# Longer expert lists in a two-layer decoder kernel, with rows of `v` copied beside their weights ahead of time

## The chip, the cores and the metric

The kernel runs on one core of a Trainium2 chip. The metric is the device time of one execution in microseconds, as the median of several runs. Seven names recur: TensorE (PE in the profile; PEld is its weight load), VectorE (DVE), ScalarE (ACT), GpSimd (POOL), SyncE (SP), and the DMA queues of SyncE, ScalarE and GpSimd (q1, q10 and q0 in the profile's list of queues).

## What is computed

The reference is a decoder trunk of two layers on 256 tokens of width 1024, all in float32. Layer 0 mixes tokens with a Mamba-2 style scan (SSD), layer 1 with block-sparse causal attention (MoBA). Behind each mixer stands a layer norm, then a mixture of very many small experts (PEER), another layer norm and a gated embedding add. The change is in the expert part:

```
def block(xb):                                   # 128 tokens
    q = (xb @ w_q).reshape(128, 8, 2, 128)       # 8 heads
    s = einsum('thcd,hcnd->thcn', q, sub_keys)   # scores against 2 x 128 keys
    ...                                          # 16 best pairs of keys per head
    expert = ...                                 # index in 0..16383
    gate = softmax(best, axis=-1)
    act = gelu(einsum('td,thkd->thk', xb, u[expert]))
    return einsum('thk,thkd->td', gate * act, v[expert])
```

Each token uses 8 x 16 = 128 of the 16384 experts. An expert has a row of `u` and a row of `v`, 1024 numbers each, in each layer.

## The kernel before, in words

**Columns.** The 16384 experts are 128 columns of 128. For every column the kernel loads the 512 KB block of `u`, splits it into a high and a low float32r part (`split`, L124: one ScalarE copy at L126, one VectorE subtraction at L127), and computes the activations of all 128 experts for all 256 tokens on TensorE (`expert_in`, L915). The gates are spread into the same shape on TensorE (`spread`, L978), where a further matmul for each token also counts which experts of the first `MANY` = 92 columns are used at all (L993), and multiplied in. Columns 0 to 91 lie in one SBUF tile, `act`, the other 36 in another, `high`.

**Output.** The output is the sum over experts of weight times row of `v`. The last 36 columns are *dense*: the whole 512 KB block of `v` is loaded by SyncE, split, and multiplied (`expert_out`, L170). A product of two split numbers takes three passes, so a dense column is 3 passes x 2 token blocks x 2 halves of the width = 12 matmuls of 512 columns (`mm3s`, L149, matmul at L152). The first 92 columns are *listed*: of their experts only those that some token uses are taken, in groups of 128. There are three kinds: used by both token blocks (12 matmuls a group), by the first only, by the second only (6 each). `CAPS` gives the number of groups that the program has for each kind: 37, 22 and 22. What does not fit raises a flag, and a fallback loop (`general`, L1212, called by `branch`) then does the surplus.

**How a group is fetched.** ScalarE's queue writes the weights of the listed columns to DRAM (`keep`, L1009): both token blocks to the table `w_d`, rows of 256 numbers, and the first block alone to `a_d`, rows of 128. For each group GpSimd then issues two indirect DMAs (`fetched`, L1175, issue at L1189): one gathers the 128 rows of weights (from `a_d` for the kind "first block only", else from `w_d`), one the 128 rows of `v`. Both are split (`group_load`, L1195) and multiplied (`group_out`, L1203).

**The listing.** `listing` (L1032) turns the counts into the row numbers for the gathers: it makes the three classes, running sums over columns (`sums`), ranks (`ranks`, L1089, two matmuls), places in the list (`places`, L1094), one equality mask and 8 tiny matmuls for each 8 columns (`place`, L1106), then sorts each row's list with rounds of "8 largest, remove them" (`order`, L1134) and computes the row numbers (`rows`, L1142). Most of it is on VectorE, and it runs beside the last 12 `expert_in` and the first `LEAD` = 6 dense columns (L1262 to L1271).

**Order of the work.** Everything is written out by position. `spread_over` gives each step of a list a place between 0 and 1, and `emit` merges the lists. The first group stage holds the 22 groups of the first block and the next `MIX` = 13 dense columns (L1290). The second holds the "both" groups, the "second block" groups, 14 dense columns, and the loads for the layer's end (L1313). Behind it come 3 held-back dense columns and the last `TAIL` = 2 groups, so that the norm of token block 0 can begin early. `pace.marks` and `after` only fix the order on an engine's queue; they add no wait.

**Buffers.** Loaded blocks go round 4 buffers `raw`, split blocks round 4 buffers `hl` (both 128 x 1024). The second group stage gathers into 6 buffers `raws` and 8 `rows_w`, which take the place of `act`.

**The mixers.** `chunk` (L132) is the way in for every weight block: a 512 KB load by SyncE and its split. The SSD mixer takes 52 chunks before layer 0's expert part, the attention mixer 30 in its own stage; then the expert part's query stage takes 16 (`query`).

## Time and profile before

Three runs took 1823.28, 1824.83 and 1824.98 us, median 1824.83. The profiled execution took 1825.7 us, of which the program's span is 1823.9 us.

| | before |
|---|---|
| profiled execution / span | 1825.7 / 1823.9 us |
| granted TensorE clock, mean | 0.999 |
| HBM read / written | 364.98 / 42.50 MB |
| layer 0's last output matmuls end near | 927 us |
| layer 1's last output matmuls end near | 1796 us |

| stage (us) | what runs |
|---|---|
| 0 to 241 | SSD mixer, then the queries of layer 0 |
| 241 to 640 | activations and gates of layer 0 |
| 640 to 680 | last activations, listing, first dense columns |
| 680 to 926 | the two group stages of layer 0 |
| 926 to 1130 | end of layer 0, attention mixer, queries of layer 1 |
| 1130 to 1497 | activations and gates of layer 1 |
| 1497 to 1545 | last activations, listing, first dense columns |
| 1545 to 1796 | the two group stages of layer 1 |
| 1796 to 1824 | end of layer 1 |

How to read the profile's rows. A group of instructions has its line, engine and operation, the tile written and the tiles read, the count, then busy time and the mean duration of one in ns, then the idle time of its engine just before them and what ended it; "issue" is idle time in which nothing that the profile shows was waited for. A row by stage has start and end, the length, then the busy time of each engine with its number of instructions, the granted clock, the share of time that the 16 DMA engines were busy (packets of several queues can overlap, so it can pass 1) and GB/s. A row of a chain of waits has a start, a length and what the time was spent on, followed back from the last instruction. A row of one line's instructions has shortest, median and longest duration in ns and the first and last start in us. A row of waits has who waited for whom, us in total, how often, and the longest.

### The profile page before, as it was taken

The page shows a single profiled execution, that of the slowest core. Times are in us where ns is not written, and L with a number is a line of the kernel's source. Part 1 is how long each engine was busy: PE and PEld are TensorE (multiplying, and loading weights), DVE is VectorE, ACT ScalarE, POOL GpSimd, SP SyncE. Part 2 cuts the span into 40 slices and gives each one's busy share as a digit, 9 for nine tenths or more (in the row PEclk, how much of TensorE's full clock was granted, in tenths as well). Part 3 has the DMA queues.
Part 4 walks back from the last instruction along what each step waited for, and adds up shares of the span by engine and source line. Part 5 has one row for each costly group of instructions (what it writes and reads, how often), then busy time and mean ns, then how long its engine had stood idle before and what let it go on. Part 6 is the DMA issues. An engine that isn't in the chain of part 4 may idle for free.

```text
span 1823.9 us, 31779 instructions
## 1 busy us (share of the span) xinstructions
PE 1806.1 (99%) x11152; PEld 1543.8 (85%) x11152; DVE 1493.5 (82%) x2948; ACT 1155.7 (63%) x2326; POOL 629.4 (35%) x608
## 2 busy tenths in 40 slices
PE   8999999999999999999999999999999999999999
PEld 7998888888888888788888788888888888887887
DVE  7798789988988997666667878998898899776675
ACT  6865556697665766565646655669666666665563
POOL 0011003332222247777700000333222224777770
PEclk9999999999999999999999999999999999999999
DMA  7655669898799998988836656989879999898880
GB/s 249 221 188 183 215 177 227 222 230 216 185 253 323 280 328 301 316 308 305 286 132 192 198 195 177 228 218 233 214 180 259 327 268 331 303 319 286 313 298 34
DMA packets 214890, 443.17 MB, mean 243 GB/s; under 512 B 18916, under 2 KB 123528, under 8 KB 213064
## 3 DMA queue, kind: packets, MB, share of 16 engines
q1 hardware_dynamic: 76360, 270.94, 45.7%
q0 software_dynamic: 66560, 133.99, 28.1%
q10 hardware_dynamic: 71808, 36.18, 6.9%
q8 instruction: 88, 1.44, 0.3%
q14 instruction: 74, 0.61, 0.1%
HBM read 364.98 MB, written 42.50 MB: 223 GB/s over the span
## 4 chain that ended last, share of the span: by engine, by line
PE 46%; DVE 4%; issue 3%; POOL 2%; ACT 2%; DMA 1%; POOLq 0%; DVEq 0%; ACTq 0%
PE acc L152 18%; PE acc L168 17%; PE acc L156 5%; PE mm L168 2%; POOL raw L1189 1%; DVE hl L127 1%; PE aux L992 1%; DMA raw<-in_v,r 1%; POOL rows_w L1189 1%; ACT hl L126 1%; PE mm L993 1%; PE mm L992 1%; PE aux L800 0%; DMA raw<-in_u 0%; DVE high L836 0%
## 5 line engine op out<-in xcount | busy, mean ns | idle before, releaser
L127 DVE TENSOR_TENSOR hl<-raw,hl 128x1024 fp32r<-128x1024 f32 x574 | 699.3, 1221 | 197.0 <-ACT hl L126 190.5
L168 PE MATMUL acc<-xT,hl 128*128 128x256 f32 (+1 forms) x4608 | 841.0, 340 | 1.5 <-DVE xT L195 0.8
L168 PEld LDWEIGHTS acc<-xT,hl 128*128 128x128 f32 x4608 | 701.1, 188 | 101.2 <-DVE hl L127 4.1
L126 ACT CAST hl<-raw 128x1024 fp32r<-128x1024 f32 x574 | 602.1, 1052 | 210.8 <-DMA raw<-in_v,r 105.3
L152 PE MATMUL acc<-hl,w 128*128 128x512 f32 x2196 | 502.2, 390 | 3.5 <-ACT hl L126 2.4
L152 PEld LDWEIGHTS acc<-hl,w 128*128 128x128 f32 x2196 | 412.5, 188 | 92.4 <-ACT hl L126 3.8
L932 POOL DMA_DIRECT2D w<-w x160 | 139.1, 869 | 400.1 <-ACT w L951 247.5
L932 POOL DMA_DIRECT2D act<-w x96 | 83.6, 871 | 302.8 <-ACT w L931 181.8
L1189 POOL DMA_INDIRECT raw<-in_v,r x132 | 153.4, 1162 | 40.2 <-issue 32.6
L930 ACT COPY w<-acc 128x256 f32<-128x256 f32 x160 | 59.8, 374 | 164.8 <-PE acc L168 159.7
L1189 POOL DMA_INDIRECT rows_w<-w_d,r x118 | 141.7, 1201 | 36.0 <-issue 32.0
L156 PE MATMUL mm<-xT,hl 128*128 128x256 f32 x816 | 100.9, 284 | 1.8 <-ACT hl L126 1.1
L156 PEld LDWEIGHTS mm<-xT,hl 128*128 128x128 f32 x816 | 98.6, 192 | 3.3 <-ACT hl L126 1.6
L931 ACT COPY w<-acc 128x256 f32<-128x256 f32 x256 | 97.3, 380 | 0.0
L930 ACT COPY act<-acc 128x256 f32<-128x256 f32 x96 | 35.7, 372 | 68.5 <-PE acc L168 68.1
L976 DVE TENSOR_TENSOR pick<-pick,r 128x2048 f16<-128x2048 f16 x64 | 78.2, 1222 | 0.9
L992 PEld LDWEIGHTS <-pick 128*128 128x128 f16 x1024 | 66.7, 98 | 14.3 <-issue 11.3
L221 POOL TENSOR_TENSOR ln_s<-ln_s,mhalf 128x1 f32<-128x1 f32 x8 | 4.4, 550 | 185.7 <-PE acc L156 130.6
L993 PE MATMUL mm<-pick 128*128 128x92 f16 x512 | 68.1, 204 | 0.0
L543 POOL TENSOR_TENSOR sq<-sq,sqt 128x256 f32<-128x256 f32 x12 | 12.5, 1040 | 150.2 <-ACT sqt L542 150.0
L992 PE MATMUL aux<-pick 128*128 128x128 f16 x688 | 59.6, 220 | 1.4 <-ACT high L1005 1.2
L1189 POOL DMA_INDIRECT pick<-a_d,r x44 | 52.2, 1187 | 14.9 <-issue 11.6
(298 smaller groups left out, 2133.2 us busy)
## 6 DMA issues: line engine op xcount, KB each, us to landing
raw<-in_u SPq DMA_DIRECT2D x256, 512.0 KB, 4.7
raw<-in_v SPq DMA_DIRECT2D x72, 512.0 KB, 5.3
w_d<-act ACTq DMA_DIRECT2D x44, 512.0 KB, 7.3
w<-w POOLq DMA_DIRECT2D x160, 128.0 KB, 5.6
raw<-in_w_q SPq DMA_DIRECT2D x32, 512.0 KB, 3.8
raw<-in_w_xbc SPq DMA_DIRECT2D x24, 512.0 KB, 4.1
act<-w POOLq DMA_DIRECT2D x96, 128.0 KB, 5.3
a_d<-act ACTq DMA_DIRECT2D x22, 512.0 KB, 10.2
```

The lines of the kernel that those rows point to most:

```text
L126: a = self.nc.scalar.copy(hi, src)
L127: b = self.nc.vector.tensor_tensor(lo, src, hi.bitcast(F32), op=OP.subtract)
L152: self.last_mm = self.nc.tensor.matmul(out, lhs(a), rhs(b), start=start and i == 0, stop=stop(n) and i == 2).ins
L156: self.last_mm = self.nc.tensor.matmul(out, lhs(a), rhs(b), start=start and i == 0, stop=stop and i == 2).ins
L168: self.nc.tensor.matmul(dst, hl[:, a, k * P:(k + 1) * P], src, start=k + a == 0, stop=(k, a) == order[-1] and k == KD - 1)
L930: nc.scalar.copy(whole, pe[:, :T])
L931: copied = nc.scalar.copy(pair[:, 1, :], pe[:, T:]).ins
L932: nc.gpsimd.dma_start(whole, pair[:, 1, :], accum_op=OP.add)
L976: nc.vector.tensor_tensor(a2, both, gates, op=OP.mult)
L992: nc.tensor.matmul(pg[:, t, :], one[:, 0, 4 * h + t], a2[:, 4 * h + t, k], start=k == 0, stop=k == 1)
L993: nc.tensor.matmul(banks["used"][:, MANY * tb:MANY * tb + MANY], one[:, 0, 4 * h + t], a2[:, 4 * h + t, 0, :MANY], start=at == 0, stop=at ...
L1189: got = nc.gpsimd.indirect_dma_start(out=dst, out_offset=None, in_=src, in_offset=rows(which))
```

## The change

The constants `MANY`, `CAPS` and `BASES` go, and each layer gets a plan: the number of listed columns, the number of *staged* columns among them, the groups of each kind, and how many of these groups are *fixed*, that is, filled from the staged columns alone:

| | listed | staged | groups (both, first, second) | fixed among them | dense columns |
|---|---|---|---|---|---|
| before, both layers | 92 | 0 | 37, 22, 22 | 0 | 36 |
| after, layer 0 | 96 | 16 | 38, 23, 23 | 6, 3, 3 | 32 |
| after, layer 1 | 104 | 40 | 42, 25, 25 | 15, 8, 8 | 24 |

For a staged column the table in DRAM has rows of 1280 numbers: the 1024 of `v`, then the 256 weights. The `v` part is copied from `v` to the table, DRAM to DRAM, 512 KB a column, on ScalarE's DMA queue (`stage`). `staging` spreads the copies over the chunks of the mixers: 16 for layer 0 over 46 chunks from the 24th chunk of the program on, 40 for layer 1 over 44 chunks from the start of the attention mixer. A fixed group then needs one gather of 5 KB rows where it needed two. In the listing, where a staged class has fewer experts than its fixed groups have room for, later ranks are moved up by the shortfall (`short`), and `order` sorts the staged and the other columns apart. A group beyond the fixed ones can still hold staged experts, so its row numbers are converted to the table's narrow rows (`rows`).

Around it: `raws` grow to rows of 1280, the tile `half` is dropped and the last group's split pair is put into two of the four `raw` buffers instead, layer 1 holds four gate matrices rather than three in the new pool, and the routing's scratch in layer 1 lies in `act`, since `high` has become too small for it.

```diff
-MANY = 92
-CAPS = (37, 22, 22)
-BASES = (0, 37, 59)
-GROUPS = sum(CAPS)
+PLANS = ((96, 16, (38, 23, 23), (6, 3, 3)), (104, 40, (42, 25, 25), (15, 8, 8)))
+WIDE = D // T + 1
...
+    def staged(self, i):
+        return self.w_d[i][:(PLANS[i][1] * P + 1) * WIDE].rearrange("(n f) t -> n (f t)", f=WIDE)
+
+    def stage(self, i, c):
+        self.nc.scalar.dma_start(self.staged(i)[1 + c * P:1 + c * P + P, :D], self.dram["v"][i, c])
+
+    def spare(self):
+        self.chunks += 1
+        while self.copies and self.chunks * self.per_copy >= self.copied + 1:
+            self.copied += 1
+            with self.after(self.pace.marks):
+                self.copies.pop(0)()
+
+    def staging(self, i, first, chunks):
+        n = PLANS[i][1]
+        self.copies = [lambda c=c: self.stage(i, c) for c in range(n)]
+        self.chunks, self.copied, self.per_copy = -first, 0, n / chunks
...
+        self.spare()
         return hl
...
                     nc.tensor.matmul(pr, every, pad[1][:, :, 64:], start=False, stop=True)
+                    if STAGED:
+                        picked["total"] = bank[:, 3 * MANY:3 * MANY + 3]
+                        nc.tensor.matmul(picked["total"], every, pad[1][:, :, 64 + STAGED], start=True, stop=True)
...
+                    if STAGED:
+                        for k in range(3):
+                            V.tensor_scalar(short[:, k:k + 1], picked["total"][:, k:k + 1], -1.0, float(FIXED[k] * P),
+                                            op0=OP.mult, op1=OP.add)
+                        V.tensor_scalar(short, short, 0.0, None, op0=OP.max)
+                        V.tensor_tensor(r[:, :, STAGED:], r[:, :, STAGED:],
+                                        short[:, :, None].to_broadcast([P, 3, MANY - STAGED]), op=OP.add)
...
                 def order(k):
-                    src = key[:, k]
-                    for n in range(0, wide[k], 8):
-                        top = best[k][:, n:n + 8]
-                        V.max(top, src)
-                        if n + 8 < wide[k]:
-                            V.match_replace(out=src, in_to_replace=top, in_values=src, imm_value=-3e38)
+                    f = FIXED[k]
+                    for hi, at, n in ((STAGED, 0, f), (MANY, f, CAPS[k] - f)):
+                        src = key[:, k, :hi]
+                        for j in range(0, n, 8):
+                            top = best[k][:, at + j:at + j + 8]
+                            V.max(top, src)
+                            if hi == STAGED or j + 8 < n:
+                                if hi == STAGED and n - j < 8:
+                                    V.memset(top[:, n - j:], 3e38)
+                                V.match_replace(out=src, in_to_replace=top, in_values=src, imm_value=-3e38)
...
-                    V.tensor_scalar(picked["w"][:, s], ids[:, s], -2.0 if k == 2 else -1.0, 1.0 if k == 2 else 0.0,
-                                    op0=OP.mult, op1=OP.add)
...
+                    near = s if k == 1 else fixed
+                    if near.start < near.stop:
+                        V.tensor_scalar(picked["w"][:, near], ids[:, near], -1.0, None, op0=OP.mult)
+                    if k != 1:
+                        at = mark[:, free]
+                        V.tensor_scalar(at, ids[:, free], 1.0 - WIDE, WIDE - 1.0, op0=OP.mult, op1=OP.add)
+                        V.scalar_tensor_tensor(at, at, float(AT - STAGED * P - 1), ids[:, free], op0=OP.min, op1=OP.subtract)
+                        V.tensor_scalar(picked["w"][:, free], at, 2.0 if k else 1.0, 1.0 if k else 0.0, op0=OP.mult, op1=OP.add)
...
+                if full:
+                    at = D + (P if kind == 2 else 0)
+                    some, parts = home[:, at:at + t], ((home[:, :D + T], staged, "w"),)
...
-            end = [group_load(s, (half, wide[1][:, 8]) if k else None) for k, s in enumerate(last)]
+            pair = tuple(self.stream.tile([P, 1024], F32R, tag="raw", bufs=4, name=self.name("hl")) for _ in range(2))
+            end = [group_load(s, pair if k else None) for k, s in enumerate(last)]
...
     def run(self):
+        self.staging(0, 24, 46)
         self.ssd()
         self.peer(0)
+        self.staging(1, 2, 44)
         self.moba()
         self.peer(1)
```

More of the change, by code (lines that the diff above doesn't have):

```diff
@@ L768, in peer @@
             column = lambda e: act[:, e, :] if e < MANY else high[:, e - MANY, :]
-            s2, s3 = (a.rearrange("p e t -> p (e t)") for a in (act[:, 64:], high))
+            far = (act[:, 64:], high) if P - MANY >= 32 else (act[:, DIRECT:DIRECT + 16], act[:, DIRECT + 16:DIRECT + 48])
+            s2, s3 = (a.rearrange("p e t -> p (e t)") for a in far)
             def spans(a, b):
@@ L909, in peer, with rows_of @@
             route += [lambda tb=tb: turn(tb) for tb in range(2)]
-            table, first = self.w_d[i], self.a_d[i]
+            table, first, staged = self.w_d[i], self.a_d[i], self.staged(i)
+            def rows_of(c, d):
+                if d <= STAGED:
+                    return staged[1 + c * P:1 + d * P, D:]
+                return table[AT + (c - STAGED) * P:AT + (d - STAGED) * P]
             now = {"ready": 0, "gated": 0}
@@ L1064, in listing @@
                 flag = picked["flag"] = take(2, 2, dt=U32)
-                wide = [-(-n // 8) * 8 for n in CAPS]
+                wide = [a - (a - n) // 8 * 8 for a, n in zip(FIXED, CAPS)]
+                short = take(1, 3, dt=F32)
                 best = [take(2, n, dt=F32) for n in wide]
@@ L1248, in peer @@
             stages = [[classes], [*sums, ranks], [], [places, ones[0]], ones[1:3], ones[3:5], ones[5:7], ones[7:9], ones[9:11],
-                      [ones[11], surplus], [keys, one], [], [two], [both]]
+                      [*ones[11:], surplus], [keys, one], [], [two], [both]]
             assert kept[0] == MANY
@@ L1272, in peer @@
             assert not lates
-            both, one, two = ([b + k for k in range(n)] for b, n in zip(BASES, CAPS))
-            last, two = two[-TAIL:], two[:-TAIL]
+            (both_s, both), (one_s, one), (two_s, two) = ((list(range(b, b + f)), list(range(b + f, b + n)))
+                                                         for b, f, n in zip(BASES, FIXED, CAPS))
+            one = [s for k in range(len(one)) for s in (one_s[k // 2:k // 2 + 1] if k % 2 == 0 else []) + one[k:k + 1]]
+            assert len(one) == CAPS[1]
+            ends = two_s or two
+            last = ends[-TAIL:]
+            del ends[-TAIL:]
             early = [tl([P, 1536], F32, "pick", 2) for _ in range(2)]
-            picked["n"], picked["order"], picked["split"] = -1, (), ()
+            picked["n"], picked["m"], picked["order"], picked["split"] = -1, -1, (), ()
             def extra(f):
@@ L1287, in emit @@
                     f(s)
-            inner = sorted(spread_over(group, both) + spread_over(group, two), key=lambda step: step[0])
+            inner = sorted(sum((spread_over(group, l) for l in (both_s, both, two_s, two)), []), key=lambda step: step[0])
             emit(spread_over(group, one), spread_over(dense, range(MANY + LEAD, MANY + LEAD + MIX)),
@@ L1319, in peer @@
             dump = tl([P, D], F32, "pick", 2)
-            gts = raws[:2]
+            gts = [raws[k][:, :D] for k in range(2)]
             self.layer_norm(0, accs[0], x, gb0, gb1, dump, pool)
```

70 lines of the change are left out of this document (44 added, 26 removed).

## The prediction

> **What bounds the kernel now.** I read the page first, then the chain of waits in order of time, then the busy time by stage, then the groups of the lines the change touches.
>
> ```profile
> span 1823.9 us, 31779 instructions
> PE 1806.1 (99%) x11152; PEld 1543.8 (85%) x11152; DVE 1493.5 (82%) x2948; ACT 1155.7 (63%) x2326; POOL 629.4 (35%) x608
> ```
> ```profile
> 769.13 156.68 PE acc L152 x690
> ...
> 1671.15 9.48 DMA raw<-in_v,r
> 1681.83 112.10 PE acc L152 x486
> ```
> ```profile
> core 0: us, PE busy (x) PEld busy (x) DVE busy (x) ACT busy (x) POOL busy (x), PEclk, DMA share, GB/s
> 95.00:184.00 89.00, 89.00 (x683) 80.24 (x682) 83.70 (x126) 53.75 (x95) 10.94 (x11) 1.00 0.58 186
> 640.00:680.00 40.00, 39.60 (x285) 32.98 (x284) 37.29 (x96) 25.04 (x51) 17.28 (x16) 1.00 1.08 321
> 737.00:926.00 189.00, 188.31 (x830) 154.79 (x829) 131.30 (x179) 111.71 (x168) 141.35 (x120) 1.00 0.86 298
> 958.00:1070.00 112.00, 111.44 (x668) 89.78 (x667) 84.73 (x185) 71.91 (x162) 1.08 (x2) 1.00 0.55 179
> 1070.00:1130.00 60.00, 59.55 (x365) 52.56 (x364) 48.04 (x149) 30.05 (x59) 1.22 (x2) 1.00 0.66 208
> 1497.00:1545.00 48.00, 47.63 (x331) 39.95 (x330) 44.98 (x118) 30.74 (x65) 19.95 (x19) 1.00 1.09 325
> 1603.00:1795.00 192.00, 189.94 (x832) 156.36 (x831) 130.90 (x178) 111.84 (x168) 139.24 (x119) 0.99 0.81 283
> ```
>
> A busy TensorE proves little alone, since matmul ends are modelled. The chain proves more: the first row is one unbroken run of 690 output matmuls in layer 0's group stage, one per 156.68/690 = 0.2271 us, with nothing else in between. So in that stage the time is the number of matmuls. Layer 1's chain leaves TensorE for the gathers: a block of `v` took 9.48 us from its issue to land (1671.15), and the run of matmuls starts again only behind it.
>
> What feeds this stage is GpSimd, which issues the gathers:
>
> ```profile
> L152 PE MATMUL acc<-hl,w 128*128 128x512 f32 x2196 | 502.2, 390 | 3.5 <-ACT hl L126 2.4 <-DVE w L127 0.8
> L1189 POOL DMA_INDIRECT raw<-in_v,r x132 | 153.4, 1162 | 40.2 <-issue 32.6 <-DMA raw<-in_v,r 3.7 <-DVE hl L127 2.4
> L1189 POOL DMA_INDIRECT rows_w<-w_d,r x118 | 141.7, 1201 | 36.0 <-issue 32.0 <-DMA raw<-in_v,r 4.0
> L1189 POOL DMA_INDIRECT pick<-a_d,r x44 | 52.2, 1187 | 14.9 <-issue 11.6 <-DMA pick<-in_v,r 1.2 <-DVE r L1138 1.1
> L1189 POOL DMA_INDIRECT pick<-in_v,r x30 | 37.0, 1233 | 17.2 <-issue 6.1 <-DVE hl L127 6.1 <-DVE w L127 4.5
> ```
> ```profile
> L1189 POOL DMA_INDIRECT raw<-in_v,r x132: 933/1150/1978, 675.6 to 1776.4; - x132
> L152 PE MATMUL acc<-hl,w x2196: 387/389/628, 666.3 to 1793.5; 128*128 128x512 f32 x200
> ```
>
> The four groups are 324 gathers, 384.3 us busy and 108.3 us idle before them, nearly all of it their own issue: 492.6/324 = 1.52 us each, back to back. That is 162 x 1.52 = 246.2 us a layer, against 1068 group-stage matmuls (all 1140 but the first six dense columns' 72) x 0.2271 = 242.5 us. TensorE and GpSimd are level, and GpSimd lives on its lead: the last gather starts at 1776.4, the last matmul at 1793.5, 17 us later. Taking matmuls away pays only if gathers go too.
>
> **The change, part by part.** *Matmuls.* A dense column or a group used by both token blocks takes 12, a group of one block 6. Before, each layer: (37 + 36) x 12 + 44 x 6 = 1140. After, layer 0: (38 + 32) x 12 + 46 x 6 = 1116; layer 1: (42 + 24) x 12 + 50 x 6 = 1092. That is 24 + 48 = 72 fewer: 72 x 0.2271 = **-16.35 us**, all on the path. The Trainium skill, page "TensorE: Matmul & The Clock Gate", section "Part 1: The HAM clock gate", gives a warm matmul of 512 columns N/2.4 GHz plus about 2.5 ns, 215.7 ns; by that the term would be -15.5 us. The trace's 227.1 ns are used.
>
> *Gathers.* A group from the staged columns needs one gather where two were: 12 such groups in layer 0, 31 in layer 1. Layer 0: 84 x 2 - 12 = 156 gathers; layer 1: 92 x 2 - 31 = 153. GpSimd saves 6 x 1.52 = 9.1 us and 9 x 1.52 = 13.7 us, where TensorE saves 5.4 and 10.9. Its lead grows by 3 to 4 us a layer, if a gather of 5 KB rows costs what the others cost. The rows bound it: 512-byte, 1 KB and 4 KB rows take 1187, 1201 and 1162 ns, so size does not show; the other end is two gathers, 3.04 us. I take 1.52. The longer lead may also remove part of the 192 - 189.94 = 2.06 us that TensorE idled in layer 1: 0 to -2.0, taken **-1.0**.
>
> *TensorE additions.* The counting matmul of the gating stage widens from 92 to 96 and 104 columns, the listing places 4 and 12 more columns:
>
> ```profile
> L993 PE MATMUL mm<-pick 128*128 128x92 f16 x512 | 68.1, 204 | 0.0
> L992 PE MATMUL aux<-pick 128*128 128x128 f16 x688 | 59.6, 220 | 1.4 <-ACT high L1005 1.2
> ```
> ```profile
> 647.10 0.35 PE L1115 MATMUL aux<-pick 128*128 128x3 f16 x8
> 647.31 0.34 PE L1115 MATMUL aux<-pick,pick 128*128 128x3 f16 x8
> ```
>
> Between 92 and 128 columns lie 16 ns, 0.44 ns a column: 256 x (4 + 12) x 0.44 ns = 1.8 us if the moving side is the limit, 0 if the weight load is. I take the middle, **+0.9**. Eight placements start 0.21 us before the next eight: 16 x 0.026 = **+0.4**; the matmul for the staged totals is one in each layer, under 0.1.
>
> *The listing on VectorE.*
>
> ```profile
> L1138 DVE MAX8 r<-r x22: 247/253/259, 662.3 to 1541.9; 128x8 f32<-128x92 f32 x22
> L1140 DVE MATCH_REPLACE8 r<-r x16: 236/240/245, 662.7 to 1541.4; 128x92 f32<-128x92 f32 x16
> L1147 DVE TENSOR_SCALAR r<-r x6: 177/178/279, 665.4 to 1543.9; 128x22 uint32<-128x22 f32 x4, 128x37 uint32<-128x37 f32 x2
> L1098 DVE TENSOR_TENSOR pick<-aux,pick x2: 445/445/445, 636.0 to 1501.4; 128x276 f32<-128x276 f32 x2
> L1112 DVE TENSOR_TENSOR pick<-iota,pick x24: 422/686/694, 639.7 to 1523.0; 128x1024 f16<-128x1024 f16 x22, 128x512 f16<-128x512 f16 x2
> ```
>
> The shortfall adds four operations of at most 0.178 and an addition of at most 0.445 us: 1.1 us a layer. The top-8 rounds go from 11 to 13 and 14; a round is 0.253 + 0.240 + about 0.09 for its value load, so 1.2 and 1.8, with some fills 1.5 and 1.9. The row numbers take 21 small operations instead of 15: 1.1. The equality masks: 0.27 (one grows from 4 to 8 columns), and 0.96 in layer 1, with a thirteenth. Sum 3.9 and 5.0 us. All of it falls where VectorE is already the fullest engine: 37.29 of 40 us, and 44.98 of 48. Its room there is 2.7 and 3.0. Behind these operations on its queue stand the splits that TensorE waits for, so I charge the overflow, 1.2 + 2.0 = **+3.2**; the bounds are 0 (the four split buffers cover it) and 8.9 (nothing does).
>
> *The copies.* 16 copies of 512 KB of `v`, DRAM to DRAM, from the middle of the first mixer on, and 40 through the second mixer and its query stage, issued on ScalarE's queue behind a split.
>
> ```profile
> q1 hardware_dynamic: 76360, 270.94, 45.7%
> q10 hardware_dynamic: 71808, 36.18, 6.9%
> ```
> ```profile
> q1 hardware_dynamic: 9588, 32.26, 58.0%
> ```
> ```profile
> ACT hl L126 <- PE acc L156: 6.9, 8, 1.7
> ACT hl L126 <- DMA raw<-in_w_q: 3.0, 1, 3.0
> ```
> ```profile
> 640.86 0.37 ACT L930 COPY w<-acc 128x256 f32<-128x256 f32 x1 [0.92 <-PE acc L168]
> 640.88 0.38 ACTq L1012 DMA_DIRECT2D w_d<-act  x1
> 641.13 0.38 ACT L931 COPY w<-acc 128x256 f32<-128x256 f32 x1
> 678.42 2.46 ACTq L1012 DMA_DIRECT2D w_d<-act  x1
> ```
>
> No DRAM-to-DRAM transfer is in the trace. 512 KB loaded cost 0.457 x 1823.9 / 270.94 x 0.524 = 1.61 us of all engines, 512 KB stored 1.82; a copy costs between 1.61 and both in series, 3.43. I take 1.82, since a load too reads and writes at once. The third row is the loads' queue from 958 to 1130 us: 58.0% of 172 = 99.8 us. With 40 x 1.82 = 72.8 it is 172.6, a share of 1.00; the listing stages ran at 1.08 and 1.09 with TensorE busy 39.60 of 40 and 47.63 of 48. There the splits wait rather for TensorE to free a buffer (6.9 us) than for a load (3.0), so loads come early and have time to give. The first mixer, at 0.58, has room for 16. On ScalarE the issue takes 0.38 us beside a running instruction (the next starts 0.27 us after the one before); where the queue was full it took 2.46. I charge **+1.0** for both; the bounds are 0 and what the rival below gives. If a staged gather waited for its copy, GpSimd would stall with all later gathers behind it; but the copies are issued some 400 us ahead.
>
> *At no cost.* The end's split pair moves into two of the stream's buffers: three matrices and the pair go round four buffers, and what is late next is one gate matrix; 0, or half a us either way.
>
> Sum: -16.35 - 1.0 + 0.9 + 0.4 + 3.2 + 1.0 = -11.85. The profiled execution took 1825.7 us (span 1823.9, 1.8 around it), 0.9 above the median of the runs, 1824.83: 1825.7 - 11.85 - 0.9 = **1813.0**. Its terms' bounds give 1807 to 1822.
>
> **The rivals.** *The copies take the loads' engines (slower).* Place: 958 to 1130 us. The largest share seen without a loss is 1.09, or 187.5 of 172 us, so the loads leave 187.5 - 99.8 = 87.7 us: the point is 87.7/40 = 2.19 us a copy. At 3.43 the demand is 237 us, 49.5 over; the splits then wait for loads and the time is 1813 + 49 = 1862. At the middle of the bounds, 2.52, it is 13 over, 1826, no change. For it: read and write both lie in DRAM, untested here. Against: nothing waits for the copies themselves, which may lag, and only the interleaved part of them delays a load. The Trainium skill, page "DMA: Bandwidth & Descriptors", section "Latency and other measured facts", gives copies between HBM tensors 214 GB/s in each direction; by that a copy takes an estimated 2.45 us, close to that middle: 98 + 99.8 - 187.5 = 10 us over, 1823. No run here shows it yet.
>
> *A wide gather costs as two (slower).* At 3.04 us GpSimd needs 84 x 3.04 = 255.4 and 92 x 3.04 = 279.7 us, TensorE (1116 - 72) x 0.2271 = 237.1 and 231.6. Past a lead of some 17 us a layer that is 1 + 31 us late: 1845. In layer 1 it decides from (231.6 + 17 - 61 x 3.04) / 31 = 2.04 us a wide gather on. The three row sizes speak against it.
>
> *The listing holds TensorE up in full:* 8.9 for 3.2, with the widened count at its end: 1820. For it: VectorE's 94%. Against: group stages ran on with four buffers, and only 0.40 us of TensorE idled in 640 to 680.
>
> *No gain.* The gathers' landing, 9.48 us in layer 1's chain, sets the stage: 1824. Against: the same bytes, 116 instead of 117 blocks of `v` a layer. That it does not do as it says, sending a surplus through the fallback loop, would be far slower; counted from the reference's inputs, 96 columns of layer 0 need 37.8, 21.8 and 21.6 groups and 104 of layer 1 40.7, 23.7 and 24.0, all under the new limits.
>
> **How the numbers follow.** Forecast 0.60 (1807 to 1818), the listing in full 0.15 (1818 to 1821), no gain 0.07, copies at the middle price 0.05, copies in series 0.08, wide gather 0.05. About 0.2%, 3.6 us, is what a measurement of this kernel can tell from no change. So faster 0.60 + 0.15 = 0.75, same 0.07 + 0.05 = 0.12, slower 0.13. The range, 1806 to 1826, holds the first four cases and leaves out the two slow ones.
>
> **What would show it.** L152's family at 2208 matmuls, 0.227 us apart; L1189's at 309 gathers, the wide ones near 1.2 us, GpSimd done well before TensorE in both layers; TensorE idle in the listing stages 1 to 2 us more than 0.4; in the second mixer a share near 1.0 and no new waits of the splits for loads. Wide gathers over 2 us, or idle TensorE between the mixer's start and the first expert, would prove me wrong.

## The result and the profile after

The changed kernel takes 1849.42 us (median of 6 runs, 1844.47 to 1856.73) against 1824.9 us (6 runs, 1819.46 to 1826.69): a ratio of 1.0137 [1.0111, 1.0163], 24.5 us slower where 11.85 us less was forecast. Its profiled execution took 1844.72 us, with a span of 1842.9, so the two profiles have 19.0 us between them to explain. Every ratio below is against runs of the kernel before on the same chip, since chips differ (on the one of the runs e5 to e8 the kernel before took 1846.39 us). Each profile is of a single execution, which can be the fastest or the slowest of its run.

The page of the changed kernel; line numbers have moved (L152 is now L171, L126/L127 are L144/L145, L168 is L187, L1189 is L1249):

```profile
span 1842.9 us, 31740 instructions
PE 1804.1 (98%) x11098; PEld 1531.2 (83%) x11098; DVE 1494.7 (81%) x2970; ACT 1152.6 (63%) x2338; POOL 611.5 (33%) x593
...
PE 59%; DMA 14%; DVE 11%; issue 7%; POOL 5%; ACT 4%; ACTq 0%; SPq 0%; POOLq 0%; DVEq 0%
...
L171 PE MATMUL acc<-hl,w 128*128 128x512 f32 x2136 | 498.0, 393 | 19.4 <-ACT hl L144 18.1
...
raw<-in_w_q SPq DMA_DIRECT2D x32, 512.0 KB, 5.7
```

The output matmuls did become fewer: this family has 2136 where it had 2196 and 12 more of the last pair under other buffer names; with the 72 from `pick` in both, 2208 for 2280. But the family's idle time grew from 3.5 to 19.4 us, ended by the split that waits for gathered data. A share of 14% of the chain lies in DMA and 7% in "issue", where the page of before has 1% and 3%.

To find where the 19.0 us lie, I cut both spans at five landmarks: the first matmul of each layer's first query, the last expert_in matmul, and the last output matmul. All times are starts of those matmuls, in us.

| stretch | before | after | difference |
|---|---|---|---|
| start to first query of layer 0 | 208.5 | 210.3 | +1.8 |
| first query to last expert_in, layer 0 | 457.7 | 458.7 | +1.0 |
| group stages, layer 0 | 261.1 | 260.9 | -0.2 |
| to first query of layer 1 (second mixer) | 144.5 | 148.5 | +4.0 |
| first query to last expert_in, layer 1 | 459.9 | 462.8 | +2.9 |
| group stages, layer 1 | 263.7 | 273.2 | +9.5 |
| tail | 28.5 | 28.5 | 0 |

Half the loss is in layer 1's group stages, which had 48 matmuls (10.9 us) less to do: some 20 us have gone there. The stage can be written as GpSimd's own stretches: a start delay, the first stage's gathers (one-block groups), the second stage's gathers, and the time from the last gather to the last matmul.

| layer 1 | before | after |
|---|---|---|
| last expert_in to first gather | 0.2 | 3.4 |
| first stage, first to last gather | 69.5 (44 gathers) | 79.9 (42) |
| second stage, first to last gather | 173.5 (118) | 170.2 (111) |
| between the stages | 1.5 | 1.2 |
| last gather to last matmul | 19.0 | 18.5 |

GpSimd's lead at the end is what it was, about 19 us. TensorE followed GpSimd, and GpSimd had its last gather out 10.0 us later after the last expert_in (254.7 against 244.7), for 9 gathers fewer.

Layer 0 went another way. There GpSimd did get ahead: its last gather starts 239.5 us after the last expert_in where it was 246.7, and its lead at the end grew from 14.5 to 21.4 us. It bought nothing, because TensorE's two long stalls lie earlier, 2.47 us at 756.21 and 1.38 at 819.37, behind a first stage that took 73.0 us for 43 gathers (70.3 for 44 before) and started 1.2 us later. From 819.37 on the chain is one unbroken row, almost to the end of the stage:

```profile
819.37 109.10 PE acc L171 x480
```

A lead that grows by the end of a stage is of no use to a stall that comes before it.

The gathers of the changed kernel by form, in both layers:

```profile
L1249 POOL DMA_INDIRECT raw<-in_v,r x111: 933/1082/1986, 678.5 to 1793.3; - x111
L1249 POOL DMA_INDIRECT rows_w<-w_d,r x96: 946/1172/1997, 744.9 to 1791.0; - x96
...
L1249 POOL DMA_INDIRECT raw<-w_d,r x32: 933/1032/1511, 759.8 to 1795.9; - x32
...
L1249 POOL DMA_INDIRECT pick<-w_d,r x11: 932/1045/3554, 670.7 to 1613.8; - x11
```

The wide gathers are the two families out of `w_d` whose target is a whole buffer (`raw<-w_d`, `pick<-w_d`). Their medians, 1032 and 1045 ns, are below the 1082 and 1172 of the narrow ones: the rival by which a wide gather costs as two is out. Two of the eleven in the last row took 3.55 us, which lifts their mean to 1.55; that isn't the width, since in the run e2 below, with the same layer 1, no wide gather took more than 2, and in e3, which has none, a narrow one took 3.94. What they wait for shows in GpSimd's timeline of the changed kernel in layer 1's first stage (start, duration, and in brackets the idle time before and what ended it):

```profile
1544.61 1.05 POOL L1249 DMA_INDIRECT pick<-w_d,r  x1 [1.27 <-DVE r L1184]
...
1556.28 1.04 POOL L1249 DMA_INDIRECT pick<-w_d,r  x1 [4.42 <-DVE r L1180]
...
1560.69 1.94 POOL L1249 DMA_INDIRECT pick<-in_v,r  x1 [1.98 <-DVE r L1201]
...
1566.68 0.94 POOL L1249 DMA_INDIRECT pick<-w_d,r  x1 [0.30 <-issue]
...
1575.45 1.89 POOL L1249 DMA_INDIRECT pick<-w_d,r  x1 [1.28 <-DVE w L145]
...
1585.58 3.55 POOL L1249 DMA_INDIRECT pick<-w_d,r  x1 [2.27 <-DVE w L145]
...
1595.66 0.93 POOL L1249 DMA_INDIRECT pick<-w_d,r  x1 [1.03 <-DMA pick<-in_v,r]
...
1604.28 0.93 POOL L1249 DMA_INDIRECT pick<-w_d,r  x1 [1.66 <-DVE hl L145]
...
1613.82 3.55 POOL L1249 DMA_INDIRECT pick<-w_d,r  x1 [2.26 <-DVE w L145]
```

Two waits are seen. The first gathers wait for VectorE's sorting and row numbers (L1180 and L1184 of `order`, L1201 of `rows`). Then four of the six wide gathers from 1566.68 on wait for VectorE to finish splitting what lay in their buffer (L145). From 1566.68 to 1613.82 there are five periods of three groups, 9.43 us each, with 5 gathers in a period. Before, the same three groups took 6 gathers, one `raw<-in_v` in each period:

```profile
1541.05 1.22 POOL L1189 DMA_INDIRECT raw<-in_v,r  x1 [0.30 <-DVE w L127]
...
1598.56 1.16 POOL L1189 DMA_INDIRECT raw<-in_v,r  x1 [0.30 <-issue]
```

These rows of the kernel before are six periods apart: 9.59 us each. One gather in six was saved and almost no time: at 1.52 us a gather, five would have taken 7.6. With 25 one-block groups in place of 22, the first stage grows by 3 x 9.43/3 = 9.4 us, where the prediction's count of gathers, 42 for 44, had it shrink by 3.

Two runs told below bear this out. In e2, with the same layer 1 and 5 gathers in a period, five periods took 44.56 us, 8.91 each. In e3, with nothing staged and 6 gathers in a period, six took 53.40 us, 8.90 each:

```profile
1559.97 0.94 POOL L1249 DMA_INDIRECT pick<-w_d,r  x1 [1.22 <-DVE w L145]
...
1604.53 1.88 POOL L1249 DMA_INDIRECT pick<-w_d,r  x1 [1.93 <-DVE w L145]
```
```profile
1565.05 0.94 POOL L1249 DMA_INDIRECT raw<-in_v,r  x1 [0.30 <-issue]
...
1618.45 1.01 POOL L1249 DMA_INDIRECT raw<-in_v,r  x1 [0.30 <-issue]
```

TensorE pays for a stall with more than its length. Its timeline in the changed kernel, where the first stage hands over to the second:

```profile
1622.94 6.35 PE L171 MATMUL acc<-hl,w 128*128 128x512 f32 x24 [1.87 <-ACT hl L144]
1632.26 11.39 PE L171 MATMUL acc<-hl,w 128*128 128x512 f32 x42 [2.97 <-ACT hl L144]
```

After the stall of 2.97 us, 42 matmuls take 11.39 us, 0.271 each instead of 0.2271: 1.85 us more. After the 1.87 us, 24 take 6.35, 0.90 more. The windows of the changed kernel (us, then TensorE's busy time, and the granted clock three columns from the end) show the mixer's stages and this place:

```profile
core 0: us, PE busy (x) PEld busy (x) DVE busy (x) ACT busy (x) POOL busy (x), PEclk, DMA share, GB/s
958.00:1070.00 112.00, 108.32 (x643) 87.76 (x642) 77.68 (x172) 66.63 (x153) 0.00 (x0) 0.98 0.87 299
1070.00:1130.00 60.00, 59.52 (x353) 51.40 (x352) 47.52 (x139) 31.08 (x57) 1.08 (x2) 1.00 0.92 316
1541.20:1814.50 273.30, 258.08 (x1098) 204.11 (x1097) 191.57 (x305) 157.66 (x245) 190.36 (x155) 0.99 0.84 288
...
1620.00:1630.00 10.00, 7.33 (x29) 4.84 (x27) 4.72 (x7) 4.05 (x7) 7.29 (x9) 1.00 1.02 353
1630.00:1640.00 10.00, 7.74 (x27) 6.31 (x28) 5.91 (x8) 5.10 (x8) 7.68 (x8) 0.83 1.01 403
1632.30:1635.60 3.30, 3.30 (x8) 2.62 (x9) 2.93 (x5) 2.50 (x5) 2.51 (x3) 0.50 1.03 415
```

In layer 1's group stages TensorE is idle for 273.3 - 258.1 = 15.2 us, and its 1092 matmuls, 248.0 us at 0.2271, fill 258.1: 10 us more go into slow ones. Only some 2 of these lie at a lower clock: of the stage's windows of 10 us only the one at 1630 shows less than 1.00, and the drop is the stretch of 0.50 behind the longer stall. The rest lies at the full clock. The Trainium skill, page "TensorE: Matmul & The Clock Gate", section "Part 1: The HAM clock gate", has the clock fall to half after an idle window of about 3.4 us. The rows agree on the half, 0.50 here; but the stall ahead of it is 2.97 us, shorter than that window, and was enough, while the one of 1.87 us was not (1.00 in 1620 to 1630). The length alone doesn't decide: in the kernel before, a stall of 1.91 us ahead of 1681.83 was followed by 0.50 from 1682.70 to 1686.10.

### The profile page after: what moved, and what is told of

Its sections match the earlier page's. It is cut to its first block, busy times and chain, and to the rows that moved or that the text cites. A ratio compares the mean times of both kernels' runs of the same rounds, so it can differ in the third digit from the quotient of the medians.

```text
span 1842.9 us, 31740 instructions
## 1 busy us (share of the span) xinstructions
PE 1804.1 (98%) x11098; PEld 1531.2 (83%) x11098; DVE 1494.7 (81%) x2970; ACT 1152.6 (63%) x2338; POOL 611.5 (33%) x593
## 4 chain that ended last, share of the span: by engine, by line
PE 59%; DMA 14%; DVE 11%; issue 7%; POOL 5%; ACT 4%; ACTq 0%; SPq 0%; POOLq 0%; DVEq 0%
PE acc L187 35%; PE acc L171 6%; PE acc L175 6%; DVE hl L145 4%; DMA raw<-in_v,r 4%; PE mm L175 3%; DMA raw<-w_d,r 2%; POOL raw L1249 2%; PE aux L1020 2%; ACT hl L144 2%; DMA pick<-w_d,r 1%; POOL rows_w L1249 1%; DMA pick<-in_v,r 1%; PE mm L1021 1%; PE mm L445 1%
## 5 line engine op out<-in xcount | busy, mean ns | idle before, releaser
L145 DVE TENSOR_TENSOR hl<-raw,hl 128x1024 fp32r<-128x1024 f32 x571 | 694.7, 1220 | 190.1 <-ACT hl L144 186.2
L187 PE MATMUL acc<-xT,hl 128*128 128x256 f32 (+1 forms) x4608 | 842.5, 340 | 2.0 <-DVE hl L145 0.6
L187 PEld LDWEIGHTS acc<-xT,hl 128*128 128x128 f32 x4608 | 700.8, 188 | 102.6 <-DVE hl L145 5.4
L144 ACT CAST hl<-raw 128x1024 fp32r<-128x1024 f32 x571 | 598.3, 1052 | 192.9 <-DMA raw<-in_v,r 92.1
L171 PE MATMUL acc<-hl,w 128*128 128x512 f32 x2136 | 498.0, 393 | 19.4 <-ACT hl L144 18.1
L171 PEld LDWEIGHTS acc<-hl,w 128*128 128x128 f32 x2136 | 398.6, 188 | 117.2 <-ACT hl L144 26.5
L1249 POOL DMA_INDIRECT raw<-in_v,r x111 | 132.2, 1191 | 35.6 <-issue 24.4
L1249 POOL DMA_INDIRECT rows_w<-w_d,r x96 | 116.9, 1218 | 29.3 <-issue 26.5
L1021 PE MATMUL mm<-pick 128*128 128x96 f16 (+1 forms) x512 | 68.4, 208 | 0.0
L999 DVE TENSOR_TENSOR pick<-iota,r 128x1024 f16<-128x1024 f16 x64 | 43.9, 685 | 11.4 <-PE aux L1020 5.2
```

The source lines that it names most:

```text
L144: a = self.nc.scalar.copy(hi, src)
L145: b = self.nc.vector.tensor_tensor(lo, src, hi.bitcast(F32), op=OP.subtract)
L171: self.last_mm = self.nc.tensor.matmul(out, lhs(a), rhs(b), start=start and i == 0, stop=stop(n) and i == 2).ins
L187: self.nc.tensor.matmul(dst, hl[:, a, k * P:(k + 1) * P], src, start=k + a == 0, stop=(k, a) == order[-1] and k == KD - 1)
L1021: nc.tensor.matmul(banks["used"][:, MANY * tb:MANY * tb + MANY], one[:, 0, 4 * h + t], a2[:, 4 * h + t, 0, :MANY], start=at == 0, stop=at ...
L1249: got = nc.gpsimd.indirect_dma_start(out=dst, out_offset=None, in_=src, in_offset=rows(which))
```

## The experiments

My theory after the result: the mechanism on TensorE held, but the group stages are set by GpSimd, which in the first stage waits for buffers and for the sorting, and in the second stage issues back to back; and the copies cost more than 1.0. The rivals: the copies do it all; the wide gather; the bytes of the gathers and not their issue.

**The copies alone.** The kernel before, with the 56 copies into a scratch that nobody reads.

```
+        self.spare_d = [self.scratch.tile([n * P, D + T], F32, name=f"spare_d{i}") for i, n in enumerate(COPIED)]
...
+        self.nc.scalar.dma_start(self.spare_d[i][c * P:c * P + P, :D], self.dram["v"][i, c])
...
+        self.staging(0, 24, 46)
...
+        self.staging(1, 2, 44)
```

> The kernel before with the 56 copies alone, at the changed kernel's places, into a DRAM tile that nobody reads. If the copies hold up the mixers' loads, as the profile after suggests (its first query of layer 0 starts 1.8 us later, its second mixer takes 4.0 us longer, layer 1's queries and activations 2.9 us longer, part of that being the wider count): the same three stages grow by about 1.8, 4 and 1.5 us and the time is 1829 to 1835 us. If they are innocent and the mixers lose for another reason: 1824 to 1826 us, and the stages stay. The group stages do not change under either theory.

1831.14 us against 1826.74, 1.0029 [1.0009, 1.0049], as the first theory had it. The first query came 1.9 us later and the second mixer took 147.9 in place of 144.5, +3.4; layer 1's group stages took 260.1, no loss. So the copies are worth some 4 to 5 us, all in the mixers, and not the rest. The page of this kernel gives the price of one, since its store queue differs from before's (6.9% of 1823.9) by the copies only:

```profile
span 1826.4 us, 31842 instructions
...
q10 hardware_dynamic: 79872, 65.54, 11.6%
```

0.116 x 1826.4 - 0.069 x 1823.9 = 86.0 us for 56 copies, 1.54 us of all engines each. That is below the bound of 1.61 in the prediction. The Trainium skill's 214 GB/s in each direction (page "DMA: Bandwidth & Descriptors", section "Latency and other measured facts"), an estimated 2.45 us a copy, is not borne out here. Yet loads wait. The waits of ScalarE in the changed kernel, 958 to 1130 us:

```profile
ACT hl L144 <- DMA raw<-in_w_q: 13.0, 5, 5.9
...
ACT act L854 <- DMA raw<-in_w_q: 6.3, 1, 6.3
...
ACT hl L144 <- DMA raw<-in_w_qk: 5.6, 2, 4.2
```

Before, such a wait was there once, 3.0 us; with the copies alone it is there as after (10.9, 5.3 and 6.6 us in the same stretch of e1). With a share of only 0.87 and 0.92, the engines are not full. But a load of `w_q` lands in a median of 5.7 us on the pages of after and of e1, in 4.2 in e3, which has no copies, and on the page of before it was

```profile
raw<-in_w_q SPq DMA_DIRECT2D x32, 512.0 KB, 3.8
```

and the chain of the changed kernel passes through loads, one of 13.06 us, and once through a copy, behind whose landing it puts SyncE's next load (the last row):

```profile
985.53 5.86 DMA raw<-in_pT
...
1024.58 13.06 DMA raw<-in_w_qk
...
1078.70 7.71 DMA w_d<-in_v
```

**Layer 1 only.** Layer 0 keeps the lists and limits of the kernel before, and nothing of it is staged.

```
-PLANS = ((96, 16, (38, 23, 23), (6, 3, 3)), (104, 40, (42, 25, 25), (15, 8, 8)))
+PLANS = ((92, 0, (37, 22, 22), (0, 0, 0)), (104, 40, (42, 25, 25), (15, 8, 8)))
```

> The changed kernel with layer 0 put back to the old lists (92 columns, nothing staged) and layer 1 as changed. If layer 1's group stage is the place of the loss (in the profiles it grew by 9.5 us where 10.9 fewer were due, against -0.2 in layer 0): 1842 to 1848 us. If both layers lose alike: about 1837 us.

1840.67 us, 1.0091 [1.0061, 1.0121], between the two expectations: most of the loss is in layer 1. By the ratios, whose intervals overlap, layer 0's part of the change costs the rest, about half a per cent, though it removes 24 matmuls; its group stages took 261.1 before and 260.9 after. The profiled execution took 1830.74 us. Its layer 1, the same program as the change's, had a first stage of 74.9 us and group stages of 265.5, so single executions scatter by several us.

**No staging.** The same lists and fewer matmuls, but two gathers for every group.

```
+PLANS = ((96, 0, (38, 23, 23), (0, 0, 0)), (104, 0, (42, 25, 25), (0, 0, 0)))
```

> The changed kernel's longer lists (96 and 104 columns, the same groups) with nothing staged: no copies, no wide gathers, two gathers for every group. By the issue theory (1.5 us a gather, back to back) the second group stages get 122 and 134 gathers instead of 113 and 111: about 14 and 35 us longer, no copies 7 us shorter, in all 1885 to 1895 us; layer 1's first group stage has 50 gathers instead of 42 and should take 12 us longer for it. By the buffer theory (the round trip of three buffers, 9.4 us for three groups, sets the first stage) layer 1's first-stage gathers span the same 78 to 80 us with 50 gathers as with 42. If the wide gathers themselves are the brake, it is faster than the changed kernel: 1835 to 1842 us.

1861.0 us, 1.0199 [1.0153, 1.0245]: slower than the change, though the intervals still overlap, and by less than the 1.52 us a gather had said (1885 to 1895). The buffer theory's part came out: layer 1's first stage took 77.9 us for 50 gathers, where the change has 79.9 for 42. Layer 1's group stages took 292.0 us. The staged columns do pay against this: 31 gathers less, 18.8 us between these two profiles. And its first gather in layer 1, too, came 3.5 us late, without any staging: there it is the longer list, not the split of the order into two. In layer 0 it came 0.5 us late, where the change has 1.7.

**More homes.** Two more buffers for the first stage's gathers, out of a tile that is already spent.

```
-                    home = early[n % 3] if n % 3 < 2 else None
+                    home = None if n % 3 == 2 else more[n % 3] if n // 3 % 2 and n >= (0, 15)[n % 3] else early[n % 3]
```

> The changed kernel with two more buffers for the first group stage, in columns of the tile high that the dense products have already used up: every second wide gather goes to the one, from the sixteenth group on every second gather of the next group to the other. Buffer theory: layer 1's first-stage gathers shrink from 80 to 65 to 70 us, the second stage starts that much earlier, and the time is 1834 to 1841 us. If gathers are paced by their issue or by the DMA engines, nothing moves: 1847 to 1851 us.

1838.45 us, 1.0073 [1.005, 1.0096], some 12 us below the change by the ratios, in the range of the buffer theory. In the profile (1832.46 us) layer 1's first stage took 72.5 us instead of 79.9, not the 65 to 70 expected; the same layer took 74.9 to 82.7 in the runs without the extra buffers and with the sorting where it was (the change, e2, e6, e9 and e11). The clearest sign is within the stage. From the sixteenth group on, with both extra buffers in use, two periods took 14.06 us, 7.03 each for 5 gathers, all issued 0.3 us apart:

```profile
1590.62 1.16 POOL L1249 DMA_INDIRECT high<-w_d,r  x1 [0.30 <-issue]
...
1604.68 1.03 POOL L1249 DMA_INDIRECT high<-w_d,r  x1 [0.30 <-issue]
```

GpSimd's waits in the whole stage (us in total, times, longest) are now mostly the sorting and the issue:

```profile
POOL pick L1249 <- DVE r L1201: 6.0, 1, 6.0
POOL pick L1249 <- issue: 5.8, 19, 0.3
POOL pick L1249 <- DVE hl L145: 4.4, 3, 2.1
```

The changed kernel's waits in the same stage, for comparison:

```profile
POOL pick L1249 <- DVE w L145: 6.4, 4, 2.3
POOL pick L1249 <- issue: 5.5, 18, 0.3
POOL pick L1249 <- DVE r L1180: 4.4, 1, 4.4
POOL pick L1249 <- DVE hl L145: 4.1, 3, 1.7
...
POOL pick L1249 <- DVE r L1201: 2.0, 1, 2.0
```

The wait for the split of the weights (L145, `w`), 6.4 us, is gone; the sorting is not.

**Late orders.** The sorting of the lists that only the second stage needs (second block, both blocks) is moved out of the last expert_in matmuls into the first group stage. It ran on two chips.

```
-                      [*ones[11:], surplus], [keys, one], [], [two], [both]]
+                      [*ones[11:], surplus], [keys, one]]
...
-                 [(0.04 + 0.1 * k, extra, f) for k, f in enumerate(todo)])
+                 [(0.04 + 0.1 * k, extra, f) for k, f in enumerate(todo)] + [(0.3, extra, two_order), (0.5, extra, both_order)])
```

> The changed kernel with the sorting of the second block's and the both lists moved from the listing stage into the middle of the first group stage (at 0.3 and 0.5 of it); they are needed only by the second. If the longer listing on VectorE holds the first groups' splits and with them the buffers (GpSimd waited 4.4 and 2.0 us for VectorE at the start of layer 1's gathers, 5.0 us in layer 0): these waits go, layer 1's first-stage gathers shrink by 5 to 7 us, and the time is 1838 to 1844 us. If only the round trip of the buffers matters: 1847 to 1851 us.

> The late sorting again, beside the changed kernel on the same chip. VectorE theory: 5 to 10 us below the changed kernel. Buffer theory: within 3 us of it, since the first stage's 9.4 us for three groups takes up what the start gains.

1856.66 us, 1.0065 [1.0033, 1.0097], and in the second run 1845.25, 1.01 [1.0077, 1.0123], beside the changed kernel on the same chip, told next. In the second run's profile (an execution of 1858.3 us) GpSimd still started layer 1's gathers 3.4 us after the last expert_in, and met the sorting later (two waits on L1180, 3.6 us): the wait moved and did not go.

**The changed kernel again**, as the mark for three others on its chip.

> The changed kernel once more, as the control for the three runs beside it on one chip: the runs with the late sorting and the plain loads met a chip on which the kernel before itself took 1846 us, so they can't be set against the changed kernel's first runs. All theories: slower than before, by 0.5% to 1.5%; less than 1.4% where the chip's gathers are slow, since it has 15 gathers fewer.

1852.15 us, 1.0144 [1.0122, 1.0166], as at first. So the late orders are worth 6.9 us beside it, which is in the range of the VectorE theory and hardly more than the two intervals leave open.

**Plain rows in half the groups.** In the second group stage, in every second group of two gathers, the gather of `v` is left out and SyncE loads a whole column of the same size instead, so these groups multiply other rows. Issue falls, bytes stay.

```
+                    if kind != 1 and not full and s % 2:
+                        parts = parts[:1]
+                        nc.sync.dma_start(raw, dram["v"][i, s])
```

> The changed kernel in whose second group stages every second group of two gathers loads a plain 512 KB block of v by SyncE in place of its gather of v (so these groups multiply other rows: the gather is left out). The same bytes move, but GpSimd issues about 25 gathers fewer a layer. If GpSimd's issue of 1.5 us a gather bounds layer 1's second stage (170 us for 111 gathers, where the matmuls need 162): that stage falls to what the matmuls need and the time by 8 to 15 us, to 1835 to 1842 us. If the DMA engines or the landing of the rows bound it: 1846 to 1851 us.

> The plain loads in place of every second gather of v in the second stages (these gathers are left out), beside the changed kernel on the same chip. Issue theory: 10 to 20 us below the changed kernel. If the movement of the bytes binds: within 3 us of it.

1834.31 us, 0.9939 [0.9909, 0.9969], and 1835.59, 1.0056 [1.0037, 1.0074], 16.6 us below the changed kernel on the same chip. Layer 1's group stages took 261.7 and 259.3 us, against 273.2 and 281.1 in the two profiles of the changed kernel; its second stage took 148.6 instead of 174.4 beside it. From 30 us into the second stage on, the chain of waits of the second run is one row:

```profile
1655.75 143.06 PE acc L171 x630
```

630 matmuls without a break, 143.06/630 = 0.2271 us each: with GpSimd relieved, TensorE is the bound again and its price is the predicted one. The bytes are the same, so the rival that the bytes set the stage is out. Nor do the plain loads land much sooner: in layer 1's second stage of e11 their median is 5.5 us from issue to landing, beside 5.8 for all gathers of e9's. And in the changed kernel's second stage GpSimd waits for little except its own issue:

```profile
POOL raw L1249 <- issue: 16.5, 54, 0.3
POOL rows_w L1249 <- issue: 11.9, 39, 0.3
```

**All trimmed, and layer 1 trimmed.** Homes and late orders with somewhat other limits, first for both layers (102 matmuls fewer than before), then for layer 1 alone.

```
+PLANS = ((96, 16, (38, 22, 22), (6, 3, 3)), (104, 40, (41, 24, 25), (15, 8, 8)))
+PLANS = ((92, 0, (37, 22, 22), (0, 0, 0)), (104, 40, (41, 24, 25), (15, 8, 8)))
```

> Both layers listed as changed, with the two extra buffers of the run with more homes, the sorting late, and lists only as long as the inputs need: 38, 22, 22 and 41, 24, 25 groups. 36 matmuls and 4 groups fewer than the changed kernel. By the buffer and VectorE theories together (8 us of matmuls, 11 of the extra buffers, 6 of the sorting): 1822 to 1828 us. If the second stages stay bound by GpSimd's issue, which loses 1 x 2 gathers there in layer 0 and 2 in layer 1: 1830 to 1836 us.

> The trimmed version with more buffers and late sorting, beside the changed kernel on the same chip: 15 to 28 us below it by the sum of the theories (8 us of matmuls, 11 of the buffers, up to 8 of VectorE), and 0 to 10 us below the kernel before; if the mixers' copies and GpSimd's issue take the rest, level with the kernel before.

> The same with layer 0 put back to the old lists: only layer 1 has 104 columns, 40 staged, 41, 24, 25 groups. 66 matmuls fewer than the kernel before (15 us), 40 copies (4 us) and the longer listing (3 us). If supply keeps up: 1815 to 1820 us. If layer 1's second stage is still bound by GpSimd (109 gathers of 1.5 us): 1822 to 1828 us.

Both layers: 1831.73 us, 0.9942 [0.9906, 0.9979], and 1827.04, 1.0009 [0.9995, 1.0023] on another chip. Layer 1 alone: 1845.09, 0.9986 [0.9959, 1.0013]. With the buffers and the sorting mended and the limits trimmed, the change comes out level on one chip and about half a per cent ahead on the other. Layer 1 alone is level with the kernel before too, as its expectation had it for a second stage still bound by GpSimd. Why the chips differ wasn't traced; where the change is ahead the kernel before itself is slower, and one trace there shows slow gathers (e8's layer 0 has the lists of the kernel before; its second stage took 187.0 us for 118 gathers, before's 174.4). Layer 1's group stages took 260.2 us in e12, 3.5 less than before with 66 matmuls (15.0 us) fewer, and the two mixers 4.5 us more. 102 matmuls are 23.2 us; the first gather 1.5 us late (3.4 with late orders alone, which fits the sorting's rounds of 8: three for 17 narrow one-block groups, two for the 16 here), the copies and a second stage still at GpSimd's rate (167.3 us for 109) give them back.

**The sum.** The change with homes, late orders and plain rows together, to see whether the causes named are all.

> The changed kernel with late sorting, two more buffers, and plain loads in place of every second gather of v in the second stages (these gathers are left out). If supply was the whole loss in the group stages, layer 1's fall to 248 to 252 us, what 1092 matmuls need, and the time is 1814 to 1819 us: 16.35 us of matmuls less than before, 5 us of copies and 1 to 3 of the listing more. If another cause is left: 1826 to 1834 us.

1828.12 us against 1827.02, 1.001 [0.9995, 1.0025]: in the range set for another cause left. Layer 1's group stages took 254.1 us, 2 us over what was expected, layer 0's 261.9, a miss. Between the two profiles, layer 1's group stages fell by 9.5 us where 10.9 were due, layer 0's grew by 0.8 where 5.4 less were due; the two mixers took 1.7 and 3.7 us more, the stretches to the last expert_in 1.2 and 1.6. The windows of its second stages and the rows of SyncE's waits in layer 0 bear on layer 0's miss:

```profile
780.00:930.00 150.00, 150.00 (x665) 124.31 (x664) 107.20 (x144) 91.34 (x136) 75.19 (x67) 1.00 0.78 271
1625.00:1795.00 170.00, 169.10 (x744) 138.31 (x743) 122.71 (x165) 104.09 (x156) 103.93 (x85) 1.00 0.83 297
```
```profile
SPq L1248 <- DMA w_d<-act: 11.6, 3, 7.5
```

TensorE is full or nearly so in both windows. In layer 0's first stage the plain loads that this experiment adds (L1248) wait up to 7.5 us for `act` to be stored, and hold dense columns' loads behind them on SyncE's queue; TensorE's two long stalls there, 2.79 us at 704.98 and 1.54 at 759.82, fit that. If so, they are the experiment's own, but this wasn't shown: the list of causes is confirmed for layer 1's group stages, to within 2 us, and stays open for layer 0's.

**Short lists, and before with plain rows.** The first is the kernel with homes and late orders, no staging, and one group less in one class of each layer, 12 matmuls and 4 gathers fewer than before; the second is the kernel before with the plain-rows edit.

```
+PLANS = ((92, 0, (37, 22, 21), (0, 0, 0)), (92, 0, (37, 21, 22), (0, 0, 0)))
```

> No staging and 92 columns in both layers, as before, with the late sorting, the two more buffers, and one group fewer in three places (37, 22, 21 and 37, 21, 22): 12 matmuls and 4 gathers fewer than the kernel before, no copies. 12 x 0.227 = 2.7 us and up to 2 us of stalls: 1820 to 1823 us. If the kernel before is bound by something else than matmuls and gathers: 1825 us.

> The kernel before with plain loads by SyncE in place of every second gather of v in its second group stages (these gathers are left out). If TensorE bounds these stages, as the prediction read the chain of waits: 1822 to 1826 us, the stages 258 to 262 us. If GpSimd's issue already bounds them: they fall below 255 us and the time below 1815 us.

1820.32 us, 0.9959 [0.9944, 0.9974], and 1820.77, 0.9963 [0.9948, 0.9977]. The first came out as expected and beats both kernels, without a copy; what the homes, the late orders and the shorter lists give each isn't separated. The second lies between its two expectations, with group stages of 260.0 and 261.9 us, the length it named for TensorE: relieved of these gathers the kernel before gains some 6 us by the ratio, so GpSimd's issue cost it something as well. TensorE and GpSimd stood about level there, as the prediction had it, and the one that stumbles sets the time.

## Why the prediction was wrong

**Matmuls, -16.35: right where TensorE is fed.** 2208 matmuls, and 0.2271 us each in the row of 630. But this term is only had if GpSimd keeps up.

**Gathers: the step that failed.** "Its lead grows by 3 to 4 us a layer, if a gather of 5 KB rows costs what the others cost." The condition held (1032 and 1045 ns) and so did the number of gathers (309). What failed is the conversion of gathers into time: it took one rate, 1.52 us, over both stages. In the first stage GpSimd is held by a second rate, three groups in 9.43 us (8.91 in e2), set by how soon VectorE has split what lies in two buffers; before, six gathers happened to take much the same, 9.59 us, so the trace of before hid it behind rows of "issue". With five gathers it came to light, and the three additional one-block groups of layer 1 cost 9.4 us instead of saving any. e3 and e4 show it: six gathers took no longer than five, and with more buffers five took 7.03 us. The prediction quoted the sign of it, 17.2 us of idle time of which 10.6 wait for splits before `pick<-in_v`, and passed over it as "nearly all of it their own issue"; of the 108.3 us in its four rows 82.3 are issue. In the second stage of layer 1 the 111 gathers took 1.53 us each, at the forecast rate, and with no lead gained in the first stage nearly every one of them was on TensorE's path; e6 and e11 show that. In layer 0 the lead did grow, by 6.9 us at the end, and paid nothing, since the stalls came before it.

**Fewer stalls, -1.0: wrong in sign.** Idle time and slow matmuls after it came to 25 us of layer 1's group stages; before, they were 263.7 - 1140 x 0.2271 = 4.8.

**Listing, +3.2 with +0.9 and +0.4 for TensorE's share: the size was about right, one effect was missed.** The stretches to the last expert_in grew by 1.0 and 2.9 us, 3.9 against 4.5. What was missed is that the sorted lists gate the gathers: GpSimd starts 1.7 us after layer 0's last expert_in and 3.4 after layer 1's, where it started 0.4 and 0.2 after it before, and it waits for the lists again at gathers soon behind. The prediction looked at the splits behind the listing on VectorE's queue and not at GpSimd, which waits for its end.

**Copies, +1.0: too low, some 4 to 5 us.** The mechanism is that of the first rival, at a small size: the loads wait, where the prediction expected "no new waits of the splits for loads". But not at the point which that rival named: a copy costs 1.54 us and the share stayed at 0.87 to 0.92. Full engines were the wrong test. What decided was a single load's landing, longer by 2 us, in a mixer where single loads stand in the chain; why a load lands later on engines that are not full was not tried.

**The rivals.** Wide gather as two: out, by the medians above. Listing in full: partly, through GpSimd. No gain from the gathers' landing: out by the plain rows, of the same size and much the same landing. The likeliest cause was missing among them: a stage paced by the round trip of its buffers.

## What to carry to other kernels

A rate read as "back to back" may be two rates that happen to coincide: before charging a producer by its count of instructions, count how many buffers it has per period and how long each takes to come free. When two engines are level, taking work from one gives nothing by itself; the time saved has to be found on the other in the same stage, not summed over the layer. And an operation that ends a dependency (a sort that gates gathers) is to be charged to whoever waits for its end, besides those queued behind it.

## What the runs showed of the hardware

A gather's cost on GpSimd showed no dependence on its rows up to 5 KB: medians of 0.9 to 1.3 us, single ones far above, and 0.30 between two. Its pace differs between executions and chips, 1.42 us in layer 1's second stage of e1, 1.47 before, 1.53 after, 1.58 in e8's layer 0, so a stage bound by gathers scatters by several us: layer 1's group stages of the changed kernel took 273.2 us in one profile and 281.1 in e9's, and 265.5 with the same layer 1 in e2's. A copy of 512 KB from DRAM to DRAM takes 1.54 us of all engines, about as much as a load. Copies lengthen the landing of loads beside them, from a median of 3.8 to 5.7 us for `w_q`, at a share of the engines of 0.85 to 0.92. And two stalls of TensorE, of 1.87 and 2.97 us, cost another 0.90 and 1.85 us in slow matmuls behind them, the second at a granted clock of 0.50.
